# A hybrid encoder block: queries, keys and values as seven half-size products, in two passes over K

## The chip, the cores and the metric

The kernel runs on one core of a Trainium2 chip. The time is that of one execution on the device in microseconds; before the change it is 1519.33 us, the median of three runs (1516.14 to 1520.48). Engines are named as the profile names them: PE is TensorE (matmuls; PEld its weight loads), DVE VectorE, ACT ScalarE, POOL GpSimd, SP the engine that issues most DMAs.

## The reference

For x of 1024 tokens x 2048 (float32), one layer:

```python
h = rmsnorm(x, norm_w)
proj = h @ w_in                                   # 2048 x 5632
q_a, k_a, v_a, g_a, q_r, k_r, v_r, g_r = split(proj)   # 1024,256,256,1024,512,512,1024,1024
attn = windowed_attention(q_a, k_a, v_a, sink, rel_bias)   # +-128 tokens, 16 heads of 64, 4 key/value heads
attn = rmsnorm(attn, attn_out_norm_w) * silu(g_a)
ret  = bidirectional_retention(rotary(q_r), rotary(k_r) / 8, v_r, decays)   # chunks of 128, 8 heads
ret  = head_groupnorm(ret, ret_gn_w) * silu(g_r)
out  = rmsnorm(x + concat(attn, ret) @ w_out, final_norm_w)
```

## The kernel before

Every large product is made of three matmuls: each float32 operand is written as a high part (rounded to `fp32r`) and a low part, and high x high, low x high and high x low are summed in PSUM. The high part of a weight tile is a cast on ScalarE (`split`, tile `wh`), the low part a subtraction on GpSimd (`wl`).

The projection's 5632 columns are worked off in units of 256 columns x 1024 tokens, K = 2048 being 16 chunks of 128:

- `STD`: six units, keys (`ka`), values (`va`) and four of queries (`qa`), with all 16 chunks, 4 banks of 512 columns x 3 matmuls each: 192 matmuls of 512 columns. The value unit has the tokens as the stationary side: 384 matmuls of 256 columns. Input rows come from `x` transposed (`xT`), times `norm_w`, split into 28 tiles `h0..h27` (and 8 tiles `r` for the last two chunks). These units do not yet know the norm of a token; `sumsq` computes it alongside, and its reciprocal root (`rcol`, and as rows `rb`, by matmuls on line 192) is multiplied in afterwards (`evac`, `k_post`).
- `FAST`: 16 units (retention's queries and keys, values, and both gates). Their first half of K is made in Strassen-like form (Winograd's): seven products of half the size instead of eight. Each product (a *slot*) is 4 chunks of 128 x 3 matmuls = 12 matmuls; a unit has 7 slots = 84 matmuls instead of 96. The left factors are sums of quarters of the weight (`prep_sums`, four GpSimd operations a unit), the right ones the 28 combined rows, which `combine()` makes on VectorE from `xT`, `norm_w` and `rb`, and sends through the DRAM buffer `cd`; a row is loaded back, cast (ACT, L1038) and its low part made (`rows_tick`). Each slot leaves its bank with `collect` (ACT copies, DVE sums); the half result goes to DRAM (`yd`). All of this is done for the 16 units one after the other, interleaved in `slot_list`.
- The second half of K of these 16 units follows as plain products (8 chunks, 96 matmuls each), at whose end the half result is loaded from `yd` and added.

Then the output projection, 16 units of seven slots again.

Around the matmuls hang queues of generators. `point()` is called after each group of 3 matmuls: it issues stores that are due, a step of `jobs` (attention and retention) each `pace[0]` points, one of `post` (what follows a unit), `side` and `gates`, and one of `aux` each `apace[0]` points. Attention is four groups (`attn_job`), a score step each of 40; it starts once `att` is done, which is set at the start of the last `STD` unit, where the tiles of the first phase are released. GpSimd's order is the written one throughout; that of PE, DVE, ACT and SP is chosen by the scheduler up to the second half of K's fifth unit, from where it is the written one too.

Of the kernel before, what the change touches and what calls it, by code (L numbers as in the profile page):

```python
# [24 lines left out]

STD = [("ka", 0), ("va", 0), ("qa", 0), ("qa", 1), ("qa", 2), ("qa", 3)]
# [7 lines left out]
NS, NF = len(STD), len(FAST)  # L34
W_STD = 8 * NS
W_ALL = W_STD + 4 * NF


@with_exitstack
def hybrid_block(ctx: ExitStack, tc: tile.TileContext, a: dict, out: bass.AP):  # L40
# [165 lines left out]
    def w_src(i):  # L206
        if i >= W_STD:
            return a["w_half"][i - W_STD]
        u, j = divmod(i, 8)
        return a["w_in"][8 * u + (j + 7) % 8 if u == NS - 1 else i]  # L210

    def w_load(i):
        if i < n_w[0] and i not in wraw and i not in wsp:
            if i < W_STD:
                r = et_("e11")
            else:
                r = rt(F32)
            SP.dma_start(r, w_src(i))
            wraw[i] = r
# [30 lines left out]
    pt, due, pace, adue, apace = [0], [0], [3.0], [0], [2.0]  # L250
# [29 lines left out]
    xraw, xrest = {}, {}  # L280
# [4 lines left out]
    def x_load(k):  # L285
        if k < NK:
            xraw[k] = t4()
            if k:
                SP.dma_start(xraw[k], a["xT"][k])
            else:  # L290
                for z in range(2):
                    SP.dma_start(xraw[k][:, 512 * z : 512 * z + 512], a["xT"][k][:, 512 * z : 512 * z + 512])

    def hx(k, part, c0, c1):
        if k < 14:
            return rows[2 * k + part][:, c0:c1]
        z = c0 // 512
        return xrest[k, part, z][:, c0 - 512 * z : c1 - 512 * z]

    def x_split(k):  # L300
        if k < NK:
            r = xraw.pop(k)
            n = nw[:, k : k + 1]
            if k >= 14:
                for z in range(2):
                    for part in range(2):
                        xrest[k, part, z] = rt(F32R)
            for z in (0, 512) if k == 0 or k >= 14 else (0,):
                z1 = z + 512 if k == 0 or k >= 14 else 1024
# [7 lines left out]
    rb = []  # L317

# [9 lines left out]
    def bias_rows():  # L328
# [6 lines left out]
        yield  # L335
# [19 lines left out]
    def sumsq():  # L355
        ssq = small(16, "ssq")
        tiles = {}
        for i in range(16 + 2):
# [3 lines left out]
            if i >= 2:  # L362
                j = i - 2
                t = tiles.pop(j)
                if j % 2:
                    A.activation(t, t, AF.Square, accum_out=ssq[:, j : j + 1])
                else:
                    V.tensor_tensor_reduce(t, t, t, 1.0, 0.0, ALU.mult, ALU.add, ssq[:, j : j + 1])
# [9 lines left out]
        rb.extend(et_("e12") for _ in range(2))  # L378
        col_to_rows(rcol, rb)
        done.add("rb")  # L380
        apace[0] = 2.7
        yield

    def decay():
# [40 lines left out]
        for h in range(8):  # L425
            t = t2()
            o = t[:, 0:128]
            V.tensor_scalar(o, ab[:, 0:128], lg[:, h : h + 1], None, ALU.mult)
            stt(V, o, ab[:, 128:256], lg[:, 8 + h : 9 + h], o, ALU.mult, ALU.add)
            A.activation(o, o, AF.Exp)  # L430
            V.tensor_scalar(o, o, 0.125, None, ALU.mult)
            store(dd[h], o, t)
            if h % 2:
                yield
        for p in range(4):
            t = t2()
            o = t[:, 0:256]
            A.activation(o[:, 0:128], ab[:, 256:384], AF.Exp, scale=lg[:, 16 + p : 17 + p])
            A.activation(o[:, 128:256], ab[:, 384:512], AF.Exp, scale=lg[:, 20 + p : 21 + p])
            store(qdd[p], o.rearrange("p (d i) -> p d i", d=2), t, (lambda: done.add("decay")) if p == 3 else None)  # L440
            if p % 2:
                yield
# [3 lines left out]
    def combine():  # L446
# [8 lines left out]
        yield  # L455
        load(1)
        yield
        for j in range(4):
            b = []
            for y in range(2):  # L460
# [4 lines left out]
                yield  # L465
            b11, b12, b21, b22 = b
            for p, x, y in ((0, b11, 0), (6, b22, 1), (1, b21, 1)):
                store(cd[4 * p + j], x, loaded[j][y])

            def less(p, x, y):  # L470
                c = out_of(stp, [128, 512], F32, "crow", 8)
                tt(V, c, x, y, ALU.subtract)
                store(cd[4 * p + j], c, c)
                return c

            c1 = less(3, b12, b11)
            yield
            c2 = less(2, b22, c1)
            yield
            less(4, b22, b12)  # L480
            yield
            less(5, b21, c2)
            if j + 2 < 4:
                load(j + 2)
            yield

    def normalise_rest():
        loaded = {}
        for i in range(8 + 2):
            if i < 8:  # L490
                loaded[i] = t4()
                SP.dma_start(loaded[i], a["xT"][8 + i])
            yield
            if i >= 2:
                x = loaded.pop(i - 2)
                for z in range(2):
                    y = x[:, 512 * z : 512 * z + 512]
                    stt(V, y, y, nw[:, 6 + i : 7 + i], rb[z], ALU.mult, ALU.mult)
                    store(xd[2 * (i - 2) + z], y, x)
                yield  # L500


    def k_post(tiles):
        while "rb" not in done:
            yield
        for b, t in enumerate(tiles):
            et, hf = b // 2, b % 2
            stt(V, t, t, 0.125, rb[hf], ALU.mult, ALU.mult)
            store(kd[128 * et : 128 * et + 128, 512 * hf : 512 * hf + 512], t, t)
            yield  # L510

    def q_post(i, tiles):
        for b, t in enumerate(tiles):
            et, hf = b // 2, b % 2
            hi = t2(F32R)
            A.copy(hi, t)
            store(qsd[2 * i + et, 0, :, 512 * hf : 512 * hf + 512], hi.bitcast(F32), hi, None, 10)
            for _ in range(3):
                yield
            tt(V, t.bitcast(F32R), t, hi.bitcast(F32), ALU.subtract)  # L520
            last = (lambda: done.add(("qa", i))) if b == 3 else None
            store(qsd[2 * i + et, 1, :, 512 * hf : 512 * hf + 512], t, t, last, 10)
            for _ in range(3):
                yield
# [123 lines left out]
    def attn_sum(g):  # L648

        for _ in range(5):  # L650
# [355 lines left out]
    def evac(u, b, p, st):  # L1006
        kind, i = STD[u]
        hf = b % 2
        d = t2()
        if kind == "va":  # L1010
            for z in range(2):
                c = rcol[:, 2 * b + z : 2 * b + z + 1]
                dz, pz = d[:, 256 * z : 256 * z + 256], p[:, 256 * z : 256 * z + 256]
                if b % 2 == 0:
                    V.tensor_scalar(dz, pz, c, None, ALU.mult)
                else:
                    A.activation(dz, pz, AF.Copy, scale=c)
# [53 lines left out]
    ticks.append(rows_tick)  # L1071
    for r in range(28):
# [14 lines left out]
    aux.append((sumsq(), 9))  # L1087
    aux.append((bias_rows(), None))
    aux.append((combine(), None))
    aux.append((bias_copies(0), None))  # L1090
# [638 lines left out]
```

## Time and profile before

| | |
|---|---|
| median of three runs | 1519.33 us (1516.14 to 1520.48) |
| the profiled execution | 1517.67 us |
| its span, first to last instruction | 1515.9 us |
| PE busy | 1461.7 us, 96% |
| POOL / DVE / ACT busy | 790.5 / 911.5 / 689.6 us |
| DMA | 353.18 MB, mean 233 GB/s |
| matmuls of `STD` (L1353 to L1355, L1346 to L1348) | starts from 6.6 to 301.2 us |
| first score matmul (L622) | 247.1 us |
| last attention matmul (L590) | 704.7 us |

Busy time is the time in which an engine runs an instruction. A matmul's own duration (0.39 us for 512 columns) is longer than the distance between two of them, since they are pipelined; the distance is what counts for the time.

### The profile page before, as it was taken

Reading aid. Unit: us, or ns where it says so; the run is one execution under the profiler, and the core shown is the slowest. Engines: PE = TensorE matmul, PEld = TensorE weight load, DVE = VectorE, ACT = ScalarE, POOL = GpSimd, SP = SyncE. Lnnn points to the kernel's source line nnn. Section 1 sums busy time; section 2 is a strip of 40 time slices with the busy share of each in tenths; the row PEclk is TensorE's granted clock in tenths of the full one; section 3 lists DMA queues with packets and bytes.
Section 4 is the critical chain, followed back from the end, with each engine's and each line's share of the span. In section 5 each row is a group of like instructions: output and inputs, shape, how many; then the busy total and the mean of one; then the engine's idle time right before and its main releaser. Section 6 shows DMA issues by size and latency. Waiting matters only on the chain.

```text
span 1515.9 us, 22190 instructions
## 1 busy us (share of the span) xinstructions
PE 1461.7 (96%) x7250; PEld 1220.7 (81%) x7250; DVE 911.5 (60%) x1827; ACT 689.6 (45%) x1465; POOL 790.5 (52%) x605
## 2 busy tenths in 40 slices
PE   8999998999999999999999999999999999999995
PEld 6898887777888888888788888878887787878774
DVE  5573333865465465566433755765667869394887
ACT  5411123766676675676212223123245345365742
POOL 3232221245545656656575756666546458475652
PEclk9999999999999999999999999999999999999998
DMA  8879889996456356455987679589379377784744
GB/s 306 283 256 328 281 263 317 295 284 211 129 164 181 123 173 170 137 166 175 324 287 253 197 247 342 197 284 318 129 265 332 114 254 262 219 312 148 269 166 161
DMA packets 225073, 353.18 MB, mean 233 GB/s; under 512 B 31884, under 2 KB 86156, under 8 KB 223549
## 3 DMA queue, kind: packets, MB, share of 16 engines
q1 hardware_dynamic: 194492, 330.78, 66.0%
q10 hardware_dynamic: 30464, 20.98, 4.4%
q8 instruction: 57, 0.93, 0.3%
q14 instruction: 60, 0.48, 0.1%
HBM read 239.97 MB, written 124.29 MB: 240 GB/s over the span
## 4 chain that ended last, share of the span: by engine, by line
PE 73%; DVE 8%; DMA 6%; issue 4%; POOL 4%; ACT 3%; SPq 1%; DVEq 0%; ACTq 0%; POOLq 0%
PE psMa L1174 5%; PE psMa L1176 5%; PE psMa L1175 5%; PE psMb L1176 4%; PE psMb L1174 4%; PE psMb L1175 4%; PE psMa L1580 4%; PE psMb L1580 4%; PE psMb L1581 4%; PE psMa L1582 4%; PE psMb L1582 4%; PE psMa L1581 4%; PE psST L605 2%; DVE h L166 2%; PE psST L1353 1%
## 5 line engine op out<-in xcount | busy, mean ns | idle before, releaser
L166 POOL TENSOR_TENSOR wl<-r,wh 128x512 fp32r<-128x512 f32 x224 | 300.7, 1344 | 403.2 <-ACT wh L172 373.9
L172 ACT CAST wh<-r 128x512 fp32r<-128x512 f32 x224 | 138.4, 619 | 231.2 <-PE psMb L1581 71.2
L1174 PE MATMUL psMa<-h,wh 128*128 128x512 f32 x512 | 202.9, 396 | 2.3 <-DVE y L166 0.8
L1176 PE MATMUL psMa<-h,wl 128*128 128x512 f32 x512 | 200.9, 392 | 2.6 <-DVE wl L166 1.9
L1175 PE MATMUL psMa<-h,wh 128*128 128x512 f32 x512 | 200.4, 391 | 0.2 <-DVE h L166 0.2
L166 POOL TENSOR_TENSOR r<-r,r 128x512 f32<-128x512 f32 x128 | 179.7, 1404 | 4.1 <-DVE wl L166 1.4
L166 POOL TENSOR_TENSOR wl<-e,wh 128x512 fp32r<-128x512 f32 x48 | 71.1, 1483 | 200.9 <-ACT wh L172 192.1
L1176 PE MATMUL psMb<-h,wl 128*128 128x512 f32 x384 | 150.9, 393 | 3.4 <-POOL wl L166 2.3
L1174 PE MATMUL psMb<-h,wh 128*128 128x512 f32 x384 | 151.8, 395 | 2.2 <-ACT e L1208 1.4
L1175 PE MATMUL psMb<-h,wh 128*128 128x512 f32 x384 | 149.9, 390 | 0.0
L166 DVE TENSOR_TENSOR h<-h 128x512 fp32r<-128x512 f32 x128 | 135.0, 1081 | 18.9 <-ACT h L1038 18.7
L166 DVE TENSOR_TENSOR e<-psMa,e 128x512 f32<-128x512 f32 x86 | 58.9, 685 | 102.4 <-PE psMa L1582 81.1
L1176 PEld LDWEIGHTS psMa<-h,wl 128*128 128x128 f32 x512 | 96.3, 188 | 26.2 <-DVE wl L166 3.2
L1174 PEld LDWEIGHTS psMa<-h,wh 128*128 128x128 f32 x512 | 96.5, 189 | 21.3 <-ACT h L1038 3.6
L1175 PEld LDWEIGHTS psMa<-h,wh 128*128 128x128 f32 x512 | 96.5, 189 | 17.6 <-DVE h L166 0.6
L1580 PE MATMUL psMa<-h,wh 128*128 128x512 f32 x256 | 104.6, 409 | 2.5 <-DVE e L166 2.5
L1580 PE MATMUL psMb<-h,wh 128*128 128x512 f32 x256 | 103.6, 405 | 0.0
L1582 PE MATMUL psMa<-h,wl 128*128 128x512 f32 x256 | 100.5, 392 | 0.0
L1581 PE MATMUL psMa<-h,wh 128*128 128x512 f32 x256 | 100.3, 392 | 0.0
L1038 ACT CAST h<-h 128x512 fp32r<-128x512 f32 x156 | 90.0, 616 | 22.5 <-DMA h<-cd 9.0
L1582 PE MATMUL psMb<-h,wl 128*128 128x512 f32 x256 | 100.1, 391 | 0.0
L1581 PE MATMUL psMb<-h,wh 128*128 128x512 f32 x256 | 100.0, 391 | 0.0
(271 smaller groups left out, 3435.4 us busy)
## 6 DMA issues: line engine op xcount, KB each, us to landing
h<-wc SPq DMA_DIRECT2D x112, 256.0 KB, 5.2
r<-in_w_fast SPq DMA_DIRECT2D x64, 256.0 KB, 3.1
r<-in_w_half SPq DMA_DIRECT2D x64, 256.0 KB, 4.8
h<-in_w_out SPq DMA_DIRECT2D x64, 256.0 KB, 5.0
e<-yd SPq DMA_DIRECT2D x64, 256.0 KB, 4.8
wc<-h SPq DMA_DIRECT2D x64, 256.0 KB, 4.6
r<-xm SPq DMA_DIRECT2D x64, 256.0 KB, 4.1
t<-in_xT SPq DMA_DIRECT2D x31, 512.0 KB, 5.7
```

Source lines behind the costliest of these rows:

```text
L166: eng.tensor_tensor(o, x, y, op)
L172: A.copy(o_hi, x)
L605: T.transpose(p[:, c0], x[:, c0], ident)
L1038: A.copy(rows[r][:, 0:512], rows[r][:, 512:1024].bitcast(F32))
L1174: T.matmul(bank, wh[:, ws], hh, start=(j == 0 and p in (0, 1, 3)), stop=False, skip_group_check=True)
L1175: T.matmul(bank, wh[:, ws], hl, start=False, stop=False, skip_group_check=True)
L1176: T.matmul(bank, wl[:, ws], hh, start=False, stop=(j == 3), skip_group_check=True)
L1353: T.matmul(p, wh[:, ws], hh, start=first, stop=False)
L1580: T.matmul(p, wh[:, ws], hh, start=(w, kk) == (0, 0), stop=False)
L1581: T.matmul(p, wh[:, ws], hl, start=False, stop=False)
L1582: T.matmul(p, wl[:, ws], hh, start=False, stop=last)
```

## The change

The six units of `STD` also become half-and-half. First their second half of K as plain products (8 chunks, 96 matmuls each, rows `h8..h23` holding the split chunks 8 to 15; `x_load` and `x_split` make only those 8 chunks); the half result goes to `yd`, for the first three units (`UNSCALED`) without `rb`. Then all 22 units run through the slots of the first half, `STD` first; a unit of `STD` asks for its half result four slots ahead (`request`), GpSimd multiplies it with `rb` where that is missing (`scale_next`), and `collect` adds each bank to it on DVE. `deliver` then hands it to `k_post`, `v_post` or `q_post`, one bank at a time; values now have columns as the stationary side like the others and are transposed on PE.

`combine()` keeps 12 of its 28 rows in place (`h0..h7`, `h24..h27`, split at once on ACT and DVE); the other 16 go through `cd` into `h8..h23` as the last plain unit leaves these. `decay` runs in the first stage, `normalise_rest` later, beside attention. At slot 7 (`OPEN`) the first phase's tiles are released and `rb` is made a second time, in the tile that later is `acc`; attention waits for keys, values, its queries and its bias. From the start to slot 20 (`FREE`) PE, DVE, ACT and SP keep the written order. Lines shift: L1353 to L1355 become L1389 to L1391, L1174 to L1176 become L1202 to L1204, the helper L166 becomes L170.

```diff
-NS, NF = len(STD), len(FAST)
-W_STD = 8 * NS
+UNSCALED = 3
+NS, NG = len(STD), len(FAST)
+NF = NS + NG
+W_STD = 4 * NS
...
-    pt, due, pace, adue, apace = [0], [0], [3.0], [0], [2.0]
+    pt, due, pace, adue, apace = [0], [0], [3.5], [0], [2.0]
...
+    def new_rb(pool, tag):
+        t = pool.tile([128, 1024], F32, tag=tag, name=nm("rb"), bufs=1)
+        rb[:] = [t[:, 0:512], t[:, 512:1024]]
         col_to_rows(rcol, rb)
...
-            for p, x, y in ((0, b11, 0), (6, b22, 1), (1, b21, 1)):
-                store(cd[4 * p + j], x, loaded[j][y])
+            quarters = [(rows[4 * p + j][:, 0:512], rows[4 * p + j][:, 512:1024], x) for p, x in ((0, b11), (6, b22), (1, b21))]
...
+            def low(hi, lo, x):
+                tt(V, lo, x, hi.bitcast(F32), ALU.subtract)
+            A.copy(quarters[0][0], b11)
             c1 = less(3, b12, b11)
             yield
+            A.copy(quarters[1][0], b22)
             c2 = less(2, b22, c1)
             yield
+            low(*quarters[0])
+            A.copy(quarters[2][0], b21)
...
+    def v_post(i, b, t):
...
+            T.transpose(p[:, 128 * c : 128 * c + 128], t[:, 128 * c : 128 * c + 128], ident)
...
+    def q_post(i, b, t):
+        et, hf = b // 2, b % 2
+        yield
+        hi = t2(F32R)
+        A.copy(hi, t)
...
+    fixed = ExitStack()
+    e = mybir.EngineType
+    fixed.enter_context(tc.manual_schedule(engines={e.PE, e.DVE, e.Activation, e.SP}))
...
-    aux.append((sumsq(), 9))
+    aux.append((sumsq(), 7))
+    aux.append((combine(), None))
...
+            if q < NS:
+                tt(V, outs[q, b], bank, outs[q, b], ALU.add)
+            else:
+                A.copy(partial(q, b), bank)
...
+    def request(q, b):
+        t = partial(q, b)
+        SP.dma_start(t, yd[q, b])
+        if q < UNSCALED:
+            unscaled.append((t, b % 2))
+            if slot[0]:
+                lag(2, scale_next)
+    def scale_next():
+        t, r = unscaled.popleft()
+        tt(G, t, t, rb[r], ALU.mult)
...
-        plain = [pS(), pS(), pT(), pO()] if u in (2, 4) else pM()
+        plain = pM()
...
-        for pos in range(NK):
+        for k in range(8):
...
+    def open_attention():
+        drain(side, "decay")
+        drain(aux, "rows")
+        flush(True)
+        ph_ctx.close()
+        phase[0] = ph_ctx.enter_context(tc.tile_pool(name="att", bufs=1, reuse_waits="tile"))
+        new_rb(phase[0], "acc")
+        done.add("att")
```

DVE, around a unit's end while `combine()` runs. `t` are tiles of `xT` or a unit's results, `crow` rows on their way to `cd`, `e`/`rb` the norm factors, `ps..` banks. Before, this is the end of the value unit:

```order
L166 TENSOR_TENSOR crow_1178<-t_151_952,crow_1149 128x512
L169 SCALAR_TENSOR_TENSOR t_170_1091<-t_170_1091,nw,e_122_709 128x512
L169 SCALAR_TENSOR_TENSOR t_170_1091<-t_170_1091,nw,e_123_710 128x512
L166 TENSOR_TENSOR crow_1217<-t_170_1091 128x512
L1015 TENSOR_SCALAR t_156_1030<-psMa_525,rcol 128x256 x2
L169 SCALAR_TENSOR_TENSOR t_171_1092<-t_171_1092,nw,e_122_709 128x512
L1015 TENSOR_SCALAR t_159_1050<-psMb_527,rcol 128x256 x2
```

And now the end of the fourth unit (`t_182` to `t_185` empty its four banks):

```order
L170 TENSOR_TENSOR crow_952<-t_162_823,t_161_822 128x512
L170 TENSOR_TENSOR h_27_134<-t_162_823,h_27_134 128x512
L170 TENSOR_TENSOR crow_968<-t_162_823,crow_941 128x512
L170 TENSOR_TENSOR h_7_114<-t_162_823,h_7_114 128x512
L173 SCALAR_TENSOR_TENSOR t_170_900<-t_170_900,nw,rb_702 128x512
L170 TENSOR_TENSOR t_182_982<-psMa_800,rb_702 128x512
L170 TENSOR_TENSOR t_183_987<-psMa_801,rb_702 128x512
L173 SCALAR_TENSOR_TENSOR t_170_900<-t_170_900,nw,rb_702 128x512
L170 TENSOR_TENSOR t_184_993<-psMb_802,rb_702 128x512
L173 SCALAR_TENSOR_TENSOR t_171_901<-t_171_901,nw,rb_702 128x512
L170 TENSOR_TENSOR t_185_999<-psMb_803,rb_702 128x512
```

The unit's four copies moved into the midst of `combine()`'s operations, which gained the low parts `h`, and all four are on DVE (in the value unit two were on ACT).

POOL, in one unit of the slots. `wl` are low parts of weights, `r` sums of weight quarters. Before, the third unit:

```order
L166 TENSOR_TENSOR r_3233<-r_3233,r_3232 128x512
L166 TENSOR_TENSOR r_3453<-r_3234,r_3233 128x512
L166 TENSOR_TENSOR wl_3465<-r_3076,wh_3464 128x512
L166 TENSOR_TENSOR wl_3506<-r_3453,wh_3505 128x512
L166 TENSOR_TENSOR r_3232<-r_3232,r_3234 128x512
L166 TENSOR_TENSOR wl_3548<-r_2900,wh_3547 128x512
L166 TENSOR_TENSOR wl_3576<-r_3232,wh_3575 128x512
L166 TENSOR_TENSOR wl_3605<-r_3233,wh_3604 128x512
```

Now the third unit (`e` are half results from `yd`):

```order
L170 TENSOR_TENSOR r_1589<-r_1589,r_1588 128x512
L170 TENSOR_TENSOR r_1682<-r_1590,r_1589 128x512
L170 TENSOR_TENSOR wl_1695<-r_1495,wh_1694 128x512
L170 TENSOR_TENSOR wl_1724<-r_1682,wh_1723 128x512
L170 TENSOR_TENSOR e_305_1659<-e_305_1659,rb_1545 128x512
L170 TENSOR_TENSOR r_1588<-r_1588,r_1590 128x512
L170 TENSOR_TENSOR wl_1745<-r_1415,wh_1744 128x512
L170 TENSOR_TENSOR e_308_1680<-e_308_1680,rb_1545 128x512
L170 TENSOR_TENSOR wl_1777<-r_1588,wh_1776 128x512
L170 TENSOR_TENSOR e_316_1714<-e_316_1714,rb_1545 128x512
L170 TENSOR_TENSOR wl_1805<-r_1589,wh_1804 128x512
```

The scalings stand between the low parts for which PE waits.

More of the change, by code (lines that the diff above doesn't have):

```diff
@@ L317, in hybrid_block, with paced @@
     rb = []
+    def paced(gen, n):
+        for r in gen:
+            for _ in range(n):
+                yield r
     def setup():
@@ L334, in bias_rows @@
         SP.dma_start(ra[0:32, :], a["rel_bias"])
-        yield
+        for _ in range(10):
+            yield
         p = pS()
@@ L357, in sumsq @@
         tiles = {}
-        for i in range(16 + 2):
+        for i in range(16 + 4):
             if i < 16:
@@ L485, in combine @@
             yield
+        done.update(("c", r) for r in (*range(8), *range(24, 28)))
+        done.add("combined")
     def normalise_rest():
         loaded = {}
[L489 to L492, printed above, removed]
+        for i in range(16 + 3):
+            if i < 16:
+                loaded[i] = t2()
+                SP.dma_start(loaded[i], a["xT"][8 + i // 2][:, 512 * (i % 2) : 512 * (i % 2) + 512])
@@ L512, in q_post @@
[L512 to L524, printed above, removed]
+            if i >= 3:
+                x, k, z = loaded.pop(i - 3), (i - 3) // 2, (i - 3) % 2
+                stt(V, x, x, nw[:, 8 + k : 9 + k], rb[z], ALU.mult, ALU.mult)
+                store(xd[i - 3], x, x)
@@ new lines, in hybrid_block, with count, k_post @@
+    finished = {}
+    def count(name):
+        finished[name] = finished.get(name, 0) + 1
+        if finished[name] == 4:
+            done.add(name)
+    def k_post(i, b, t):
+        et, hf = b // 2, b % 2
+        yield
+        A.activation(t, t, AF.Copy, scale=0.125)
+        store(kd[128 * et : 128 * et + 128, 512 * hf : 512 * hf + 512], t, t, lambda: count("ka"))
+        yield
+    def v_post(i, b, t):
+        et, hf = b // 2, b % 2
+        yield
+        yield
+        p = pT()
+        for c in range(4):
+            T.transpose(p[:, 128 * c : 128 * c + 128], t[:, 128 * c : 128 * c + 128], ident)
+        yield
+        o = t2()
+        A.copy(o, p)
+        o4 = o.rearrange("p (c g d) -> p g c d", c=4, g=2)
+        for g in range(2):
+            last = (lambda: count("va")) if g else None
+            store(vd[2 * et + g, :, 4 * hf : 4 * hf + 4, :], o4[:, g], o, last)
+        yield
@@ L527, in hybrid_block @@
+    def q_post(i, b, t):
+        et, hf = b // 2, b % 2
+        yield
+        hi = t2(F32R)
+        A.copy(hi, t)
+        store(qsd[2 * i + et, 0, :, 512 * hf : 512 * hf + 512], hi.bitcast(F32), hi, None, 10)
+        for _ in range(3):
+            yield
+        tt(V, t.bitcast(F32R), t, hi.bitcast(F32), ALU.subtract)
+        store(qsd[2 * i + et, 1, :, 512 * hf : 512 * hf + 512], t, t, lambda: count(("qa", i)), 10)
+        yield
     acc = [None]
@@ L1100, in attention @@
         if g == 1:
[L1101 to L1102 removed]
+            pace[0] = 2.5
+        yield ready("ka", "va", ("qa", g), ("bias", g), "att")
         yield from attn_job(g)
@@ L1330, in hybrid_block @@
                     raw_load(0, x)
-            elif last_u and pos == 13:
+                for r in range(8, 24):
+                    todo.append((pt[0] + 4 * ((r - 8) // 2 + 1) + 1, ("c", r), r, cd[r]))
+            elif last_u and k == 5:
                 prep_sums(0, 0)
                 prep_sums(0, 1)
-            elif last_u and pos in (12, 14):
-                prep(*slots[pos // 2 - 6])
+            if last_u and k in (4, 6):
+                prep(*slots[k // 2 - 2])
+            if (u, k) == (NS - 2, 2):
+                for x in asked.pop(-1):
+                    request(*x)
+            elif u == NS - 2 and k > 4 and unscaled:
+                scale_next()
@@ L1397, in hybrid_block @@
         slot[0] = n
+        step[0] = 16 * NS
+        if n == OPEN:
+            open_attention()
+        elif n == FREE:
+            fixed.close()
+        for x in asked.pop(n, ()):
+            request(*x)
         prepare(q, p, 0)
```

245 lines of the change are left out of this document (98 added, 147 removed).

## The prediction

> **What bounds the kernel now.** I read the page's busy table first, then stretches, then the waits at the one place where TensorE stands still.
>
> ```profile
> span 1515.9 us, 22190 instructions
> PE 1461.7 (96%) x7250; PEld 1220.7 (81%) x7250; DVE 911.5 (60%) x1827; ACT 689.6 (45%) x1465; POOL 790.5 (52%) x605
> ```
>
> TensorE is busy 96% of the span, so time is won by issuing fewer matmuls or by closing its few gaps. The next view is busy time by stretch (length, then each engine's busy us with its instruction count, granted clock, DMA share, GB/s).
>
> ```profile
> 80.00:96.00 16.00, 16.00 (x135) 16.00 (x135) 10.03 (x13) 1.86 (x3) 8.73 (x3) 1.00 0.60 183
> 100.00:170.00 70.00, 70.00 (x325) 58.59 (x324) 29.89 (x40) 12.51 (x22) 17.79 (x14) 1.00 0.96 321
> 155.00:225.00 70.00, 70.00 (x310) 57.98 (x310) 24.03 (x69) 16.60 (x39) 16.98 (x13) 1.00 0.82 272
> 106.00:350.00 244.00, 232.74 (x1087) 192.82 (x1086) 124.61 (x292) 98.66 (x227) 65.98 (x51) 0.99 0.89 291
> 240.00:360.00 120.00, 107.49 (x545) 89.29 (x545) 78.57 (x200) 78.86 (x188) 39.67 (x30) 0.99 0.89 286
> 258.00:263.00 5.00, 4.33 (x13) 3.48 (x13) 3.77 (x11) 3.67 (x9) 0.00 (x0) 0.66 0.95 327
> 357.00:705.00 348.00, 143.83 (x364) 68.38 (x364) 1.00 0.51 156
> ```
>
> Four readings. A 512-wide product costs 70.00/310 = 0.2258 us (query unit, 155 to 225); a 256-wide one of the value unit 16.00/135 = 0.1185. Between 240 and 360, where attention opens beside the last full unit, TensorE idles 12.5 us, and from 258 to 263 its clock is 0.66, another 0.34 x 5 = 1.7 us. DMA is the second resource of the first 350 us: 291 GB/s from 106 to 350, 321 over the best 70 us. The last row counts line 1174 alone: 364 of each of three product lines, so attention's three later groups cost TensorE (348 - 3 x 364 x 0.2258)/3 = 34 us each. The waits between 240 and 350 (who, on whom, us, times, longest):
>
> ```profile
> DVE h L166 <- ACT h L1038: 9.9, 11, 5.0
> PE psST L622 <- DVE nmx L631: 9.0, 6, 4.4
> ACT h L1038 <- DMA h<-cd: 9.0, 5, 4.5
> ```
>
> Score matmuls (L622) wait for VectorE, which waits for ScalarE's row conversions, which wait for the `cd` rows: 28 rows are converted while attention starts.
>
> **The change, term by term.** The sum is made against the profiled execution, 1517.67 us (span 1515.9), which is 1.66 below the median of the runs shown.
>
> 1. *Matmuls, -18.4.* Before: five units x 192 wide products and one of 384 narrow: 960 x 0.2258 + 384 x 0.1185 = 262.3 us. After: six units x 8 chunks x 12 = 576, and 6 x 84 = 504: 1080 x 0.2258 = 243.9.
>
> 2. *Work added on TensorE, +4.1.* The row broadcast of the norm factors is done once more, and values, now made transposed, need 16 transposes. The chain of the span has the broadcast:
>
> ```profile
> 55.41 5.75 DMA t<-in_x
> 61.27 0.87 ACT t L366
> 71.52 0.18 DVE rcol L166
> 71.74 2.05 PE psST L192 x16
> ```
>
> It costs 2.05; 16 transposes at 2.05/16 another 2.05.
>
> 3. *The opening of attention, -12.7.* By the order the first score matmul now stands behind 390 of the seven-product matmuls, well into unit 4 (units count from 0); 12 rows are made in place, and the last of 16 conversions stands in unit 1. The coupling above has no partner left there. Of 12.5 + 1.7 = 14.2 I leave 1.5. Bounds: 0 (it comes along) and -14.2.
>
> 4. *Norm factors earlier, +1.4.* The broadcast stands behind 252 matmuls: 6.6 + 252 x 0.2258 = 63.5 us (6.6: the first matmul's wait, row below). Before, `rcol` was ready 71.5, 10.3 after the last `x` tile landed (61.2). After, 4.2 MB of `xT` no longer go ahead of `x`; the last `x` load stands behind 201 matmuls, but may issue from 174 on: 46 to 52 us, landed 52 to 58, `rcol` 62 to 68. TensorE waits 0 to 4.6 us, where it waits 1.0 now; I take 2.4, near the middle.
>
> ```profile
> PE psST L192 <- DVE rcol L166: 1.0, 1, 1.0
> ```
>
> The next rows are groups (busy us, mean ns, then idle before and its releaser):
>
> ```profile
> L1353 PE MATMUL psMa<-h,wh 128*128 128x512 f32 x84 | 34.1, 406 | 6.6 <-DVE h L314 6.6
> L166 DVE TENSOR_TENSOR e<-psMa,e 128x512 f32<-128x512 f32 x86 | 58.9, 685 | 102.4 <-PE psMa L1582 81.1 <-PE psMa L1176 18.4 <-ACT P L635 1.2
> ```
>
> 5. *combine() in front of the unit ends, +5.* Its 32 + 12 VectorE operations now run beside units 2 to 4, each of which ends by emptying the same four PSUM banks into which the next unit writes at once (before, alternate units took other banks). Ahead of unit 3's first copy the order has 36 VectorE rows since combine() began. Their pitch is in the timeline:
>
> ```profile
> 73.56 3.60 DVE L169 SCALAR_TENSOR_TENSOR t<-t,e 128x512 f32<-128x512 f32 x4 [1.87 <-ACT e L200]
> ...
> 86.09 1.67 DVE L166 TENSOR_TENSOR crow<-t,crow 128x512 f32<-128x512 f32 x1
> ...
> 89.39 0.68 DVE L166 TENSOR_TENSOR crow<-t,crow 128x512 f32<-128x512 f32 x1
> ```
>
> 21 operations from 73.56 to 90.07: 0.786 us each. combine() starts when its `xT` tiles land, about 72 (broadcast at 66, and a 512 KB load lands after 5.7):
>
> ```profile
> t<-in_xT SPq DMA_DIRECT2D x31, 512.0 KB, 5.7
> ```
>
> 72 + 36 x 0.786 = 100.3; four copies of 0.685 with two operations between: 104.6. TensorE ends unit 3 at 6.6 + 384 x 0.2258 + 2.05 + 2.4 = 97.8 and needs the fourth bank 2.0 later: 4.8 late, taken as 5. Bounds: 0 (pitch 0.68, the short row) and 10 (tiles landing at 77). Queued behind the waiting operations on ScalarE are the casts of the next weights, so the wait shows on TensorE either as a bank or as weights, once; on SP the `cd` stores wait too, ahead of weight loads that are asked for three tiles (72 matmuls, 16 us) before their split.
>
> 6. *GpSimd, +1.5.* In units 1 and 2 of the products it makes 7 low halves, 4 weight sums and, new, 4 scalings of a half result with `rb`; the nearest row to the last is e<-e,h:
>
> ```profile
> L166 POOL TENSOR_TENSOR wl<-r,wh 128x512 fp32r<-128x512 f32 x224 | 300.7, 1344 | 403.2 <-ACT wh L172 373.9 <-PE psST L605 5.3 <-DMA h<-wc 4.1
> L166 POOL TENSOR_TENSOR r<-r,r 128x512 f32<-128x512 f32 x128 | 179.7, 1404 | 4.1 <-DVE wl L166 1.4
> L166 POOL TENSOR_TENSOR e<-e,h 128x512 f32<-128x512 f32 x32 | 46.3, 1457 | 18.0 <-DVE t L1269 18.0
> ```
>
> One VectorE operation of combine(), by tile (duration min/median/max in ns):
>
> ```profile
> L166 DVE TENSOR_TENSOR crow<-t,crow x8: 672/682/1674, 81.6 to 112.8; 128x512 f32<-128x512 f32 x8
> ```
>
> 7 x 1.344 + 4 x 1.404 + 4 x 1.457 = 20.9 us beside 84 x 0.2258 = 19.0: 1.9 short in each unit, 3.8 in two. Weights are prepared two slots (5.4 us) ahead, which hides most of it: 1.5, bounds 0 and 7. The upper end stands in the last row: the same VectorE operation takes 0.68 us or 1.67, beside a GpSimd operation. The Trainium skill (SBUF — State Buffer, Who interferes with whom) says that a VectorE instruction with two SBUF inputs and a GpSimd instruction that reads SBUF shut each other out for a whole instruction; the trace agrees. By that rule some ten row conversions would each take up to 0.68 us from GpSimd in these units, this term would be 7, and the sum 1509.
>
> 7. *DMA, +3.* Bytes in all stay about the same (353 MB), but come sooner. From the end of unit 3 to the end of the first attention group (matmuls 396 to 1296) the order issues 297 SP transfers, with ScalarE's 75.6 MB by their shapes, while TensorE needs 900 x 0.2258 + 34 + 2 = 239 us: 316 GB/s. Middle of 291 and 321, 306 GB/s, gives 247, 8 late. Queries and weights are fetched some 5 us before they are used, so 3 remain. Bounds: 0 (321) and 16 (291). Late, they stop TensorE through the weights or through VectorE's sums with `yd`.
>
> Extra VectorE and ScalarE work elsewhere costs nothing: seven sums of 0.685 a unit lie under 19 us of products. The last 1159 us keep their work.
>
> Sum: -18.4 + 4.1 - 12.7 + 1.4 + 5 + 1.5 + 3 = -16.1: 1501.6 for a profiled execution, 1503 for the median.
>
> **Rivals.**
> - *The queue is full and slower than before (the other side).* At 275 GB/s the 75.6 MB take 275 us, 275 - 239 - 5 = 31 late: 1503 + 28 = 1531. For: 316 GB/s are asked of a queue that gave 291, and it holds small pieces (queries, values, bias). Against: 321 for 70 us without a TensorE wait. It makes the kernel slower from 24 us late, 75.6 MB/268 us = 282 GB/s downward. Chance 0.08.
> - *The queue stays at 291*: 16 late instead of 3: 1516, no difference. 0.10.
> - *The opening's stalls come along*, since VectorE and ScalarE still feed attention, sums and conversions there: term 3 about -2, 1514. For: L622's waits are on VectorE. Against: groups 2 to 4 of attention run beside the same products with PE busy nearly throughout. 0.10, half of it within 0.3%.
> - *GpSimd bound in units 1 and 2*: 1509. 0.10.
> - *All of it hidden*: terms 4 to 7 zero and 14.2 regained: 1519 - 18.4 + 4.1 - 14.2 = 1491. For: DMA's 321, VectorE's 0.68. Against: the in-order chain of term 5. 0.17. The Trainium skill (HBM Reference, Specifications) puts a core's share at about 358 GB/s, and a core alone higher; by 358 term 7 alone would be 0 and the time 1500. No stretch of 70 us here exceeds 321.
> - *The forecast*, 1496 to 1510: 0.45.
>
> **How the numbers follow.** 0.3% is 4.6 us, about what a measurement of this kernel tells from no change. Faster (below 1514.8): 0.45 + 0.17 + 0.10 + 0.05 = 0.77; same: 0.10 + 0.05 = 0.15; slower 0.08. The range reaches from just under the hidden case to the queue at 291: 1489 to 1517.
>
> **What would show it.** TensorE: 1080 wide products in place of 960 wide and 384 narrow ones, still 0.2258 apart. Term 3: few waits of score matmuls on `nmx`. Term 5: waits on the copies or on `wl` near 98 us. Term 6: GpSimd over 95% busy between about 160 and 205 us. Term 7: DMA over 300 GB/s from 110 to 350. I am wrong if matmul waits in the first 360 us exceed 45 us.

## The result, and the profile after

The changed kernel takes 1507.76 us (median of four runs, 1507.19 to 1510.86), the kernel before in the same comparison 1519.07: a ratio of 0.9941, 95% interval 0.9921 to 0.996. It is faster by 11 us, of 16 forecast, and inside the range. In a second comparison the same program gave a ratio of 0.9899 (0.988 to 0.9917), 14.7 us; by the two intervals the gain lies between 6 and 18 us. The two intervals do not overlap, so an interval does not cover all that differs from one comparison to the next. The profiled execution took 1507.27 us.

The page's first lines, of the changed kernel:

```profile
span 1505.5 us, 21951 instructions
...
PE 1451.6 (96%) x7018; PEld 1201.1 (80%) x7018; DVE 941.8 (63%) x1851; ACT 697.1 (46%) x1483; POOL 860.3 (57%) x659
```

TensorE has 232 matmuls and 10.1 busy us less, nearly what the span lost (10.4); its idle time is as long as before (53.9 against 54.2), but lies elsewhere. Busy time by stretch, columns as before:

```profile
52.00:62.00 10.00, 7.46 (x26) 5.45 (x25) 8.86 (x19) 6.43 (x16) 2.55 (x2) 0.83 1.03 398
151.00:242.00 91.00, 91.00 (x419) 75.60 (x418) 43.93 (x59) 36.14 (x62) 74.86 (x56) 1.00 0.95 309
160.00:205.00 45.00, 45.00 (x215) 37.52 (x214) 15.91 (x24) 16.82 (x29) 41.93 (x32) 1.00 0.96 314
106.00:350.00 244.00, 238.25 (x1140) 197.42 (x1139) 140.53 (x268) 112.85 (x237) 153.91 (x115) 1.00 0.92 304
240.00:360.00 120.00, 112.90 (x577) 94.83 (x576) 81.62 (x201) 73.58 (x175) 64.22 (x48) 0.99 0.92 298
```

From 151 to 242, where the first of the seven-product units run (they last to about 277), TensorE never idles. Around 55 it stops and then runs at a lower clock. Beside the first group of attention it idles 7.1 us where it idled 12.5. TensorE's longest waits up to 360 us:

```profile
PE psMa L1389 <- DVE h L305: 6.5, 1, 6.5
PE psO L629 <- DVE PTl L170: 3.7, 3, 1.8
PE psMa L1389 <- ACT t L1053: 2.5, 1, 2.5
PE psMa L1389 <- ACT h L487: 1.5, 1, 1.5
PE psO L629 <- DVE P L668: 1.4, 1, 1.4
PE psST L661 <- DVE nmx L670: 1.2, 1, 1.2
```

The first line is the start of the kernel. The third and fourth are the ends of units 1 and 3 of the first stage. The others belong to attention: the wait on `nmx`, 10.3 us before (L622 there), is 1.2; new are waits of the output matmuls (L629) on transposed probabilities.

**The end of unit 1 (52.9 us).** ScalarE's timeline (start, duration, then idle before and its releaser):

```profile
54.16 1.06 ACT L363 ACTIVATE t<-t 128x1024 f32<-128x1024 f32 x1 [1.27 <-DMA t<-in_x]
55.12 0.19 ACT L363 ACTIVATION_READ_ACCUMULATOR t<-t 128x1 f32 x1
55.22 0.57 ACT L1053 COPY t<-psMa 128x512 f32<-128x512 f32 x1
```

The bank's copy (L1053) stands behind a square of the norm (L363), which waits for an `x` tile. Unit 2 needs that bank. TensorE starts again at 55.84.

**The end of unit 3 (102.7 us).** VectorE's timeline; its next row empties the first bank:

```profile
102.55 0.68 DVE L170 TENSOR_TENSOR h<-t,h 128x512 fp32r<-128x512 f32 x1
103.15 0.74 DVE L173 SCALAR_TENSOR_TENSOR t<-t,nw,rb 128x512 f32<-128x512 f32 x1
103.82 1.28 DVE L170 TENSOR_TENSOR t<-psMa,rb 128x512 f32<-128x512 f32 x2
```

This is the forecast wait behind `combine()`. The list of waits names ScalarE's `h` (L487) as the releaser, but what ends just before TensorE goes on is the emptying of the first bank: it is free at 104.5, and TensorE goes on at 104.64.

**Attention.** VectorE again:

```profile
297.42 1.05 DVE L173 SCALAR_TENSOR_TENSOR t<-t,nw,rb 128x512 f32<-128x512 f32 x1 [3.58 <-DMA t<-in_xT]
...
316.68 0.84 DVE L173 SCALAR_TENSOR_TENSOR t<-t,nw,rb 128x512 f32<-128x512 f32 x1 [2.95 <-DMA t<-in_xT]
...
325.17 1.17 DVE L173 SCALAR_TENSOR_TENSOR t<-t,nw,rb 128x512 f32<-128x512 f32 x1 [3.23 <-DMA t<-in_xT]
```

It stands for tiles of `normalise_rest`; the score and probability steps are queued behind. TensorE issues its last matmul before a stop at 298.8, 302.6, 317.6 and 325.2.

### The profile page after: what moved, and what is told of

The parts are those of the page before. It is cut to its first block, busy times and chain, and to the rows that moved or that the text cites. A ratio compares the mean times of both kernels' runs of the same rounds, so it can differ in the third digit from the quotient of the medians.

```text
span 1505.5 us, 21951 instructions
## 1 busy us (share of the span) xinstructions
PE 1451.6 (96%) x7018; PEld 1201.1 (80%) x7018; DVE 941.8 (63%) x1851; ACT 697.1 (46%) x1483; POOL 860.3 (57%) x659
## 4 chain that ended last, share of the span: by engine, by line
PE 64%; DVE 12%; DMA 11%; issue 5%; POOL 4%; ACT 2%; SPq 2%; DVEq 0%; POOLq 0%; ACTq 0%
PE psMa L1204 5%; PE psMa L1202 5%; PE psMa L1203 5%; PE psMb L1204 4%; PE psMb L1202 4%; PE psMb L1203 4%; PE psMa L1633 4%; PE psMb L1633 3%; PE psMa L1635 3%; PE psMa L1634 3%; PE psMb L1635 3%; PE psMb L1634 3%; DVE h L170 2%; DMA t<-mpd 2%; PE psST L644 2%
## 5 line engine op out<-in xcount | busy, mean ns | idle before, releaser
L170 POOL TENSOR_TENSOR wl<-r,wh 128x512 fp32r<-128x512 f32 x290 | 393.4, 1358 | 516.2 <-ACT wh L176 477.9
L176 ACT CAST wh<-r 128x512 fp32r<-128x512 f32 x290 | 179.0, 618 | 304.0 <-PE psMb L1634 64.3
L1202 PE MATMUL psMa<-h,wh 128*128 128x512 f32 x608 | 241.5, 397 | 1.5 <-DVE y L170 0.7
L1204 PE MATMUL psMa<-h,wl 128*128 128x512 f32 x608 | 239.3, 394 | 2.6 <-DVE wl L170 1.9
L1203 PE MATMUL psMa<-h,wh 128*128 128x512 f32 x608 | 238.8, 393 | 0.2 <-DVE h L170 0.2
L170 POOL TENSOR_TENSOR r<-r,r 128x512 f32<-128x512 f32 x152 | 213.3, 1404 | 4.5 <-DVE wl L170 1.3
L1204 PE MATMUL psMb<-h,wl 128*128 128x512 f32 x456 | 179.9, 395 | 5.1 <-DVE wl L170 3.0
L1202 PE MATMUL psMb<-h,wh 128*128 128x512 f32 x456 | 180.5, 396 | 1.6 <-ACT wh L176 1.0
L1203 PE MATMUL psMb<-h,wh 128*128 128x512 f32 x456 | 178.6, 392 | 0.0
L170 DVE TENSOR_TENSOR e<-psMa,e 128x512 f32<-128x512 f32 x110 | 75.4, 686 | 114.7 <-PE psMa L1635 58.8
L1204 PEld LDWEIGHTS psMa<-h,wl 128*128 128x128 f32 x608 | 114.9, 189 | 30.1 <-DVE wl L170 3.2
L170 DVE TENSOR_TENSOR h<-h 128x512 fp32r<-128x512 f32 x116 | 127.7, 1131 | 14.0 <-ACT h L1065 13.2
L1202 PEld LDWEIGHTS psMa<-h,wh 128*128 128x128 f32 x608 | 115.4, 190 | 23.7 <-ACT h L1065 2.4
L1203 PEld LDWEIGHTS psMa<-h,wh 128*128 128x128 f32 x608 | 115.2, 190 | 21.2 <-DVE h L170 0.6
L170 DVE TENSOR_TENSOR e<-psMb,e 128x512 f32<-128x512 f32 x109 | 74.3, 686 | 57.2 <-PE psMb L1204 45.2
L1204 PEld LDWEIGHTS psMb<-h,wl 128*128 128x128 f32 x456 | 85.8, 188 | 27.7 <-DVE wl L170 4.8
L1633 PE MATMUL psMa<-h,wh 128*128 128x512 f32 x256 | 104.6, 409 | 2.6 <-DVE e L170 2.6
L1633 PE MATMUL psMb<-h,wh 128*128 128x512 f32 x256 | 103.6, 405 | 0.0
L1635 PE MATMUL psMa<-h,wl 128*128 128x512 f32 x256 | 100.6, 393 | 0.0
L1634 PE MATMUL psMa<-h,wh 128*128 128x512 f32 x256 | 100.4, 392 | 0.0
L1202 PEld LDWEIGHTS psMb<-h,wh 128*128 128x128 f32 x456 | 86.0, 189 | 18.1 <-ACT wh L176 1.9
```

Source lines behind the costliest of these rows:

```text
L170: eng.tensor_tensor(o, x, y, op)
L176: A.copy(o_hi, x)
L1202: T.matmul(bank, wh[:, ws], hh, start=(j == 0 and p in (0, 1, 3)), stop=False, skip_group_check=True)
L1203: T.matmul(bank, wh[:, ws], hl, start=False, stop=False, skip_group_check=True)
L1204: T.matmul(bank, wl[:, ws], hh, start=False, stop=(j == 3), skip_group_check=True)
L1633: T.matmul(p, wh[:, ws], hh, start=(w, kk) == (0, 0), stop=False)
```

## The experiments

Each was compared with the kernel before on the same chip. The table gives the ratio and, from the trace, five lengths in us. Wide products (512 columns, of the large matrix products) are counted in TensorE's timeline; a length is the distance of two starts. "To 400" is the start of the 400th (counted from 0), "400-576" holds the one matmul of the bias table (line 334), "816-1050" the start of attention, "1130-1296" the rest of its first group, "last 1400" the end of the second half of K (56 products) and the whole output projection.

| kernel | ratio (95%) | to 400 | 400-576 | 816-1050 | 1130-1296 | last 1400 |
|---|---|---|---|---|---|---|
| changed | 0.9941 (0.9921-0.996) | 109.4 | 41.1 | 59.9 | 59.6 | 367.0 |
| again | 0.9899 (0.988-0.9917) | 107.6 | 41.1 | 60.5 | 61.7 | 365.7 |
| banks | 0.9935 (0.9913-0.9956) | 103.9 | 47.8 | 60.4 | 63.2 | 365.6 |
| norm | 0.9991 (0.9976-1.0006) | 110.1 | 41.1 | 80.5 | 54.0 | 365.0 |
| both | 1.0001 (0.9988-1.0015) | 101.9 | 47.9 | 79.6 | 56.2 | 367.0 |
| banks2 | 0.9906 (0.9882-0.9931) | 102.4 | 41.1 | 59.2 | 60.3 | 362.8 |
| ahead | 0.9941 (0.992-0.9962) | 109.8 | 41.2 | 60.3 | 61.0 | 365.9 |
| copies | 0.9957 (0.994-0.9974) | 110.0 | 41.1 | 58.7 | 59.9 | 365.5 |
| nostt | 0.9913 (0.9889-0.9937) | 110.7 | 41.1 | 59.8 | 56.9 | 365.0 |
| tail | 0.9931 (0.9907-0.9954) | 108.6 | 41.1 | 60.1 | 60.9 | 366.7 |
| pool | 0.9902 (0.9881-0.9922) | 103.0 | 41.1 | 59.9 | 60.8 | 366.5 |
| best | 0.9888 (0.9864-0.9911) | 103.4 | 41.1 | 59.9 | 59.7 | 364.7 |

Between kernels that an edit leaves alone there, the lengths differ by 0.1 us (400-576), 1 to 2 (816-1050), 3 (to 400) and 4 (the last two columns). Each comes from one profile. The ratios' intervals are 4 to 7 us wide, so the lengths say more on where time went; a difference in a length counts where it is larger than these figures.

**again**: the changed kernel, unedited.

> The changed kernel once more, for its time and a second profile. From the start of the second half of K on, the changed kernel was 7.2 us slower than the kernel before in the first profile at its end (stretch from the last product of that half to the end of the span: 366.9 us against 359.7), though most of the rows stand in the same order there. Theory 'the tail is the change's': the stretch takes 366.9 again, within 0.5, with the same stalls. Rival 'the tail is chance': it takes something else between 360 and 367, and the stalls lie elsewhere. Time 1508 in both.

From the last product of the second half of K to the end of the span it took 365.6 us against 366.9, with the same large stops. That is outside the 0.5 us named and within the rival's range, but the stalls are the theory's. The time was 1503.27, lower than expected.

**before_again**: the kernel before, unedited, one execution.

> The kernel before once more, for a second profile. Theory 'the tail is the change's': the stretch from the last product of the second half of K to the end of the span takes 359.7 again, within 1, against 365.0 to 367.0 in the five profiles of the changed kernel and its variants. Rival 'chance': it lies among those, at 363 or more.

The stretch took 361.6 us (one execution, 1522.47). It missed the theory's bound of 1 us and the rival's 363 too, and lies below all twelve profiles in the table, by 1 us at the least. The mean of the table's last column is 365.6, some 4 to 6 us above the two profiles of the kernel before; that is what the change costs there, and not the 7.2 of the first pair.

**banks**: what the reuse of banks costs in the first stage.

```diff
-        plain = pM()
+        plain = [pS(), pS(), pT(), pO()] if u in (1, 3) else pM()
```

> Units 1 and 3 of the first stage take the four other PSUM banks, so that the next unit need not wait for the emptying of theirs. Theory 'banks': the stop of 2.7 us at 52.9, the 1.9 us that follow at half clock, and the 2.8 us from 102.7 to 108 go, 7.4 in all, to about 1500.5; the row broadcast comes at about 66.8 and its factors are ready at 66.1. Rival 'given back': the row broadcast or the following unit then waits for the same norm squares and rows, and the time stays within 2 us of 1508.

The stops at both unit ends went: the 400th product started 3.7 us sooner than in *again*. Then TensorE reached the bias matmul some 4 us earlier and stood there as long (first line: waits from 100 to 130 in *banks*; then SP's timeline in *banks* and in *again*):

```profile
PE psST L334 <- DMA ra<-in_rel_bias: 4.0, 1, 4.0
```

```profile
113.80 0.33 SPq L330 DMA_DIRECT2D ra<-in_rel_bias  x1
```

```profile
113.43 0.33 SPq L330 DMA_DIRECT2D ra<-in_rel_bias  x1
```

The load is issued at the same time in both, since SP first issues stores of `combine()`'s rows, for which it waits 11 us. It takes 4 to 5 us to land, and the unedited kernel arrives about 1 us after it. The theory's stops are shown. The rival, "given back", has the total, but not by its mechanism: what takes the gain back is the bias table, and not norm squares or rows.

**banks2**: the same, with that matmul ten steps later.

```diff
-        for _ in range(10):
+        for _ in range(20):
             yield
         p = pS()
```

> The other banks for units 1 and 3, and the one matmul of the bias table (line 334) twenty steps behind its load and not ten. With the banks alone TensorE reached that matmul 4.3 us sooner and stood 4.4 us for the table, whose load SP issues behind the stores of VectorE's differences, and then ran at half clock. Theory 'banks': without that stop the 3.7 us gained up to the 400th product stay: 1503.3 - 3.7 = 1499.6. Rival 'the next one': a wait for rows or weights takes the place of this one, and it stays at 1502 to 1505.

There is no stop at the bias matmul, and 5.2 us are gained at the 576th product (143.5 against 148.7). The ratio does not show it: 3.4 us went at 558 us, at an output matmul of attention behind a VectorE sum that waits for `mpd` tiles (the halves of attention's result, read back), and 2.7 in the second half of K, where the clock was lower (last section). By the trace the theory holds to the 576th product. The rival has the total (1504.93), but neither a wait for rows nor one for weights took the place of the stop.

**norm**: `normalise_rest` ahead of three of the four bias copies.

```diff
             aux.append((bias_copies(g), None))
-        aux.append((normalise_rest(), None))
+            if g == 0:
+                aux.append((normalise_rest(), None))
```

> The normalised second-half rows are made behind the first group's bias instead of behind all four, so 13 of 16 stand on VectorE ahead of the first score and 3 behind it. Theory 'late tiles': the stops of score and output matmuls between 298 and 327 (1.33 + 1.48 + 0.76 + 1.56 = 5.1 us) come from VectorE standing in front of a late xT tile, and most of them go: 1503. Rival 'attention's own chain': TensorE stops there just as long, for nmx, P and PTl, since VectorE and ScalarE are the pace of the first group: 1508. Second rival 'moved': VectorE now stands for xT tiles between 185 and 235 and holds up the sums that empty the slots' banks, 1508 or more.

The theory's stops went, and more was lost elsewhere. Beside attention the length fell to 54.0 us from 59.6 and 61.7 in the two profiles of the changed kernel, and TensorE was busy 59.64 of 60 us (first row *norm*, where these products run some 20 us later; second row *again*):

```profile
310.00:370.00 60.00, 59.64 (x318) 50.80 (x317) 33.49 (x95) 39.49 (x95) 30.70 (x24) 1.00 0.88 275
```

```profile
290.00:350.00 60.00, 54.50 (x280) 45.99 (x279) 41.83 (x100) 33.96 (x82) 30.09 (x22) 0.97 0.89 290
```

But 20 us were lost ahead of it (816-1050), in two stops with half clock behind each. The waits of *norm*, from 200 to 300 and, for SP, from 200 to 265:

```profile
ACT wh L176 <- DMA r<-in_w_fast: 15.9, 4, 5.8
...
PE psMb L1202 <- ACT wh L176: 6.6, 1, 6.6
...
ACT t L557 <- DMA xd<-t: 5.3, 2, 3.0
...
PE psMa L1202 <- ACT wh L176: 4.8, 1, 4.8
```

```profile
SPq L118 <- ACT t L557: 16.0, 6, 4.4
```

Read from below: SP stands 16 us for ScalarE's conversions of queries (L557), to store them. Those wait for a buffer whose `xd` store has not landed; the new rows share these buffers. Weight loads stand behind SP's store, `wh` (the high part of the weights) comes late, and TensorE stops. So the second rival had the time, but not the place: TensorE waits for weights, and not for VectorE to empty the slots' banks. From 230 to 270, where this happens, the DMA moved 288 and 311 GB/s in two halves, about the 309 of a stretch without stops. That speaks for the order in one queue, and not for its bytes; *copies* below tests that.

**both**: *banks* and *norm* together.

> Both edits, the other banks and the earlier normalised rows. If both theories hold the gains add up: 7.4 + 5.1 = 12.5, to about 1495.5. If they share a limit behind them (the DMA queue, attention's start), less than the larger of the two single gains is added: 1500 or more.

Both losses are there again (47.9 at the bias matmul, 79.6 at the start of attention), and so are both gains (101.9 to the 400th product, 56.2 beside attention). The total is that of *norm* within the intervals, so nothing is left of what *banks* gained early.

**ahead**: the tiles asked for earlier.

```diff
-        for i in range(16 + 3):
+        for i in range(16 + 5):
...
-            if i >= 3:
+            if i >= 5:
```

> The normalised second-half rows stay where they are, but each xT tile is asked for five steps ahead and not three. Theory 'late tiles': VectorE no longer stands in front of them, and the stops of TensorE between 297 and 330, with the half clock behind them some 7 us, shrink by 4 or more: 1496 to 1499. Rival 'ring': the tiles come from the same six buffers as the stores of queries and rows, so that asking sooner makes SP stand for those, as with the earlier rows, where SP stood 16 us for ScalarE's conversions and the weights behind it came late: 1505 or more.

Its median, 1509.09, lies where the rival put it, but its ratio is that of the changed kernel's first comparison, so the time decides nothing. VectorE stood just as long, 10.8 us for these tiles from 285 to 345 against 10.2 in *again*, and the lengths did not change. So asking sooner is no cure: SP's wait ahead of such a load (L515; *ahead*, 285 to 330) is for a buffer whose earlier `xd` store has not landed:

```profile
SPq L515 <- DMA xd<-t: 4.3, 5, 1.9
```

In *again* it is 6.6 us in six waits. So the rival's buffers are seen; SP's long wait for ScalarE (16 us in *norm*) did not come back, and with it the rival's price.

**copies**: 48 copies of 256 KB taken out of the first 360 us. Read and written they are 25 MB; the profile's figures for the queue count a copy once, 12.6 MB.

```diff
-    side.append((w_copies(), None))
...
+        elif n == 66:
+            side.append((w_copies(), None))
...
-            plan.append((8 * n, SP.dma_start, ...
+            plan.append((7 * n, G.dma_start, ...
```

> The 48 copies of the output weight (25 MB read and written) are issued by GpSimd from slot 66 on, about 370 us, and no longer by SP from 107 to 365. Theory 'order, not bytes': the first 360 us stop for single late transfers behind SP's waits and not for bandwidth; the time stays within 2 us of 1503. Rival 'bytes': with 25 MB of some 75 gone the xT tiles and weights land sooner, and the stops of the first attention group go too: 1498 or less. Second rival 'GpSimd': its 48 issues beside the weights' low halves cost TensorE, 1506 or more.

From 106 to 350 the queue now moved 257 GB/s instead of 304 (300 in *again*), some 11 MB less:

```profile
106.00:350.00 244.00, 239.06 (x1143) 198.17 (x1142) 145.40 (x269) 113.48 (x238) 157.74 (x115) 1.00 0.80 257
```

The 1296th product started at 352.9, in *again* at 354.1 and in the first profile at 353.2. The start up to the first copy (105 us) differs by chance; from the 400th to the 1296th product it took 242.9 us, against 246.5 and 243.8. So these copies are worth 0.9 to 3.6 us there, less than the 5 of "bytes". VectorE still stands 8.1 us for the `xT` tiles from 285 to 345, for 10.2. This speaks for "order, not bytes", but a small share of bytes is not excluded.

The time, 1512.87, is the second rival's: from the 576th to the 2424th product it took 574.7 us against 565.8. That GpSimd's issues are the cause is not shown. TensorE's waits in *copies* from 353 to 727 us:

```profile
PE psST L661 <- DVE nmx L670: 4.3, 5, 1.8
PE psO L629 <- DVE PTl L170: 4.2, 6, 3.2
...
PE psMb L1204 <- POOL wl L170: 0.6, 1, 0.6
```

Only 0.6 us is a wait for a low half. The rest is attention's, and the longest stop, 3.2 us at 570, is in *banks2* and *nostt* too, where no copy was moved.

**nostt**: VectorE's part of `normalise_rest` left out.

```diff
-                stt(V, x, x, nw[:, 8 + k : 9 + k], rb[z], ALU.mult, ALU.mult)
                 store(xd[i - 3], x, x)
```

> The sixteen second-half rows go from xT to DRAM as they are: VectorE's multiplication by the norm weight and factor (16 operations) is left out, every transfer stays. Theory 'VectorE stands in front of late tiles': TensorE's stops between 297 and 330 go, and the stretch from the 1130th to the 1296th product takes 54 us (53.9 with the earlier rows) and not 61.7; time about 1503.3 - 7 = 1496. Rival 'attention's own chain of nmx, P and PTl': the stretch stays within 1.5 us of 61.7, and the time at 1503.

The stops from 297 to 330 went, and the length fell to 56.9, below every profile in which these operations stand there: by 4.8 against *again*, of 7.7 expected, and by 2.7 against the first profile. One stop of 2.2 us is left at 341 (VectorE's timeline):

```profile
341.77 0.69 DVE L170 TENSOR_TENSOR t<-t,t 128x512 f32<-128x512 f32 x1 [4.73 <-DMA yd<-e]
```

This is the first sum of attention's halves, standing for its `mpd` tiles: another late tile in front of attention's steps. (The view names a store of `yd`; the second of the two `mpd` tiles landed at 341.7.) The total, 1504.87, did not follow, for 3.4 us went again at the sum near 562 and 2.7 in the second half of K, as in *banks2*.

**tail**: the final norm's Newton step on ScalarE.

```diff
-        newton(t, v, y)
-        tt(V, y, y, t, ALU.mult)
+        A.activation(t, v, AF.Copy, scale=y)
+        A.activation(t, t, AF.Copy, scale=y)
+        A.activation(t, t, AF.Copy, scale=-0.5, bias=1.5)
+        A.activation(y, y, AF.Copy, scale=t)
```

> The four one-column operations of the final norm's Newton step (128x1), of which some take 0.16 us and some 1.24 on VectorE beside a GpSimd operation, are made on ScalarE. Theory 'port': the stop of 2.0 us before a weight's low half, 166 products from the end, and the half clock behind it go; the last 166 products take 41.2 us, as in the kernel before, and not 44.0: 1500. Rival 'ScalarE late': its steps stand behind casts that wait for GpSimd, VectorE's products with them come later still, and the time is 1503 to 1506.

In *again*, VectorE and GpSimd at the disputed place:

```profile
1437.65 1.24 DVE L170 TENSOR_TENSOR ft<-fv,fy 128x1 f32<-128x1 f32 x1
1438.92 1.22 DVE L170 TENSOR_TENSOR ft<-ft,fy 128x1 f32<-128x1 f32 x1
1440.17 0.15 DVE L189 TENSOR_SCALAR ft<-ft 128x1 f32<-128x1 f32 x1
1440.36 1.03 DVE L170 TENSOR_TENSOR fy<-fy,ft 128x1 f32<-128x1 f32 x1
```

```profile
1437.58 1.29 POOL L170 TENSOR_TENSOR r<-r,r 128x512 f32<-128x512 f32 x1
1438.83 1.29 POOL L170 TENSOR_TENSOR wl<-r,wh 128x512 fp32r<-128x512 f32 x1
1440.07 2.67 POOL L170 TENSOR_TENSOR r<-r,r 128x512 f32<-128x512 f32 x2
```

Operations on one column, with two inputs, end when the GpSimd operation beside them ends; the one with a single input takes 0.15 us. In the kernel before, whose order here is the same, only the first of the three is long (1.24, and then 0.16 twice), since GpSimd stands still when the others start. With the steps on ScalarE the stretch around that stop took 15.65 us (66 products), as before (15.68), and not 18.87. The last 166 took 42.5 for 44.0, but some 3 were lost 680 products from the end, at a late cast 110 us ahead of the moved steps. The stop is explained; the kernel gained nothing (1506.66).

**pool**: *banks2*, with the sums of attention's halves on GpSimd.

```diff
-                tt(V, x, x, y, ALU.add)
+                tt(G, x, x, y, ALU.add)
```

> Other banks, the bias matmul twenty steps behind its load, and the sixteen sums of attention's halves (mpd) on GpSimd and not VectorE. Theory: VectorE's standing for mpd tiles (3.6 us at 555, 3.4 near 340) goes from in front of attention's PTl and nmx; the stretch from the 1800th to the 2100th product takes 100.4 us and not 105.2, and the time is about 1499. Rival 'moved': GpSimd stands for the same tiles, the weights' low halves behind them come late, and the time stays at 1505 or more.

The stop at 558 went, but the stretch named took 104.1 us and not 100.4: TensorE now waits there three times for ScalarE's `PTh` (2.2 us in all), as it did not before. From the 576th to the 2424th product 2.4 us of *banks2*'s 3.0 came back (566.4, 568.8, *again* 565.8). The time, 1503.66, lies between the theory and the rival.

**best**: *pool* and *tail*.

> The same with the Newton steps on ScalarE. If every theory holds: 1503.3 - 5.2 (early stops, up to the 576th product) - 2.8 (tail) = 1495.3. Rival 'phases': small shifts elsewhere (the second half of K and the output product differ by 1 to 3 us from variant to variant) eat part of it: 1498 to 1504.

1500.39, the lowest median, but its interval overlaps that of *again*. At the start of the second half of K it led by 4.8 us (709.7 against 714.5), and 4.0 of these went in that half, 3.4 by the clock (last section). That is the rival's "phases". That it beats the changed kernel is not shown.

## Why the prediction was right, point by point

| term | forecast | measured |
|---|---|---|
| 1 matmuls | -18.4 | -18.4, no stop from 151 to 242 |
| 2 broadcast, transposes | +4.1 | +3.2 |
| 3 attention's opening | -12.7 | -5.4 |
| 4 norm factors | +1.4 | +3.2 |
| 5 `combine()` | +5 | +2.8 |
| 6 GpSimd | +1.5 | +0.5 |
| 7 DMA | +3 | 0 (no wait on a load of weights) |
| 360 us on | 0 | +4.1 (-1.7, -1.4, +7.2) |
| sum | -16.1 | -10.0; span -10.4 |

*Terms 1 and 2* were right. The distance of two products is as before. The broadcast of the norm factors has 16 starts 0.11 us apart, 1.8 in all, and the transposes take 1.4.

*Term 3* was mis-sized, and its step failed: 5.4 us of idle time came back, of 12.7. The partner of the old stall was gone, as said: the wait on `nmx` fell from 10.3 to 1.2. But I let attention open beside nothing, while the change puts `normalise_rest` there, and costed VectorE's extra work at nothing by its length. It is not its length that stops TensorE, but that it stands for a DMA with attention's steps behind it. *norm* and *nostt* show that: against the two profiles of the changed kernel 5.6 and 7.7 us went in the one, 2.7 and 4.8 in the other.

*Term 4.* The broadcast did not wait (1.0 saved): the factors were ready at 66.1 and it began at 71.2. The late `x` tiles cost at another place, the end of unit 1: 2.5 us of waiting, and 0.17 of the clock over 10 us, 1.7. I had asked who waits for the factors, and not what stands behind the squares on ScalarE.

*Term 5* had its mechanism and place right. The emptying of the first bank began at 103.82, not 100.3: the 36 rows began at 74.14 and not 72, and stood 0.82 us apart and not 0.786. TensorE came later too, at 103.0 and not 97.8, so 2.8 remained (stretch from the 252nd to the 400th product: 36.5, with other banks 33.7).

*Terms 6 and 7* cost next to nothing. GpSimd was 93% busy from 160 to 205 (41.93 of 45 us), just under the 95% named, and yet the one wait on `wl` in 360 us came to 0.5. The Trainium skill (SBUF — State Buffer, Who interferes with whom) would have made term 6 7 us, by VectorE's row conversions; the lock exists, as *tail* shows, but in these units its cost lay within the two slots of lead. DMA gave 304 GB/s from 106 to 350, as the sign asked, and 309 where TensorE did not wait once; *copies* prices 12.6 MB of the queue at 0.9 to 3.6 us, which come through waits that term 3 counts already.

*The rest.* "The last 1159 us keep their work" held for the work and not for the time. Attention's later groups left TensorE 2.9 us idle (357 to 716) for 4.6 before. The second half of K took 422.7 us for 424.1, which is the clock and not the change (last section). The stretch behind it took 7.2 longer, in the repeats 4. The stop 166 products from the end is a matter of how VectorE and GpSimd fall together; the rest is not explained.

So the direction and the size of term 1, which carries the gain, were right by their mechanism, but that 1503 came so near is in part luck: a gain sized 7 us too high, term 4, 2 us too cheap, and a loss of 4 us left out stood against terms 2, 5, 6 and 7, which were 7 us too dear together.

## What to carry to other kernels

Before moving work beside a latency chain, ask of each instruction which transfer it waits for and what is queued behind it on that engine; its length is the smaller part. An early stop removed is worth something only up to the next instruction that depends on a fixed time, a load or a store in an ordered queue: follow the gain from stretch to stretch. And where two engines' small operations fall together by chance, a change that touches neither can move the time by 2 to 3 us.

## What the hardware showed that I had not expected

A stop of 2.1 us can be enough for TensorE's clock to fall. *again*, TensorE:

```profile
326.54 0.39 PE L629 MATMUL psO<-PTl,k 128*128 128x256 f32 x1 [2.13 <-DVE P L668]
...
328.68 0.63 PE L1202 MATMUL psMa<-h,wh 128*128 128x512 f32 x1
329.11 0.63 PE L1203 MATMUL psMa<-h,wh 128*128 128x512 f32 x1
```

From half a microsecond after it, for 3.4 us (327.0 to 330.4), the granted clock is 0.50, and wide products start 0.43 us apart and not 0.226. The Trainium skill (TensorE: Matmul & The Clock Gate, Part 1) names an idle window of about 3.4 us for this; here stops of 1.8 to 2.5 us did it several times, and the measurement decides.

It does not happen each time. In every run TensorE stops for some 2 us (1.7 to 2.4) at the same place in the second half of K, for a sum of VectorE. The nine microseconds behind that stop in *before*, the changed kernel's first profile and *again*:

```profile
991.08:1000.08 9.00, 9.00 (x33) 7.20 (x34) 5.96 (x16) 3.19 (x7) 4.13 (x3) 0.62 0.69 233
```

```profile
975.15:984.15 9.00, 9.00 (x41) 7.12 (x42) 6.71 (x17) 3.78 (x8) 4.59 (x4) 0.81 0.66 223
```

```profile
973.46:982.46 9.00, 8.58 (x47) 6.87 (x48) 7.44 (x18) 3.98 (x9) 6.17 (x5) 1.00 0.71 205
```

The clock cost 3.4 us, 1.7 and nothing (0.38, 0.19 and 0 of 9 us), and the half took 424.1, 422.7 and 421.5. In *banks2*, *copies*, *nostt*, *pool* and *best* it was 0.62 as well. So a difference of some 3 us between two runs of the same rows need not have a cause in the kernel's order.

The DMA moved 398 GB/s from 52 to 62 us. The 321 that I had taken as the most was that of 70 us; over ten, the kernel before had reached 408 too (42 to 52 us).
